# Nine pairs of weight strips of a mixer's input projection, each pair as seven half-size block products

## The chip, the cores and the metric

The kernel runs on one core of a Trainium2 chip. The metric is the device time of one execution in microseconds, as the median of several runs. Engines: TensorE (matmuls, "PE" in the profile; its weight loads are "PEld"), VectorE ("DVE"), ScalarE ("ACT"), GpSimd ("POOL") and SyncE ("SP"), which issues nearly all transfers to and from the memory, in one queue and in order.

## The reference

One decoder layer over 1024 rows of 1024 features, all in float32:

```python
f1 = swiglu(rms_norm(h, ffn1_pre_g[l]), ffn1_w_in[l], ffn1_w_out[l])
h = h + HALF_STEP * rms_norm(f1, ffn1_post_g[l])

u = rms_norm(h, mix_pre_g[l])
p_rwkv, p_swa, q_mem, gate_logits = _split(u @ w_in[l], IN_SIZES)
...
g_a, g_b, g_c = _split(jax.nn.sigmoid(gate_logits + gate_b[l]), (D, D, D))
merged = (g_a * (y_a @ w_branch[l, 0]) + g_b * (y_b @ w_branch[l, 1])
          + g_c * (y_c @ w_branch[l, 2]))
h = h + rms_norm(merged @ w_out[l], mix_post_g[l])

f2 = swiglu(rms_norm(h, ffn2_pre_g[l]), ffn2_w_in[l], ffn2_w_out[l])
h = h + HALF_STEP * rms_norm(f2, ffn2_post_g[l])
```

`swiglu` has an inner width of 2816. `y_a` is a recurrent mixing of rows (RWKV-7), `y_b` attention in a window of 128 with 8 query heads, `y_c` attention to 256 memory rows. The change is in `u @ w_in[l]`: its output has 48 strips of 128 columns. Strips 0 to 13 feed the recurrence, 14 to 19 the window attention (`p_swa`), 20 to 23 are the memory queries, and 24 to 47 the gates ("gate 0" is strip 24).

## The kernel before, in words

**Operands.** A float32 product is made of three matmuls. Each weight strip of 128 x 512 is loaded (`w_raw`), rounded by ScalarE to `w_hi` (L288) and its rest `w_lo` subtracted by VectorE (L290); activations are split the same way (`split`, L472 and L473). `mm3` (L364 to L366) multiplies hi by hi, hi by lo and lo by hi into one PSUM tile of 128 x 512. A strip of `w_in` has 8 row blocks of the inner dimension and two halves of the rows, so it takes 8 x 2 x 3 = 48 matmuls. `plan` writes the order of all weight strips down in one list; loads, roundings and subtractions run up to eight operands ahead of the matmuls that use them.

**Half-size products.** The two feed-forward blocks (ffn1, ffn2) already take two strips at once: of the four quarter blocks of the weights and of the activations, sums and differences are formed, so that seven products of 12 matmuls (`product`) do the work of eight. In ffn1's and ffn2's input stage the sums of the weights are formed as the strips arrive; 22 pairs run there, 19 us each (84 matmuls). For the output weights of ffn1 and ffn2 the sums are formed once, in units of four loads, four VectorE operations and four stores to `ffn1_sum_d` and `ffn2_sum_d` (`sums_loads`, `sums_made`): eleven units of ffn1 beside its input pairs 9 to 19 (tiles `ws`, L655 to L658), eleven of ffn2 in the attention stage and the branches (`sums_beside`, tiles `gin`).

**The mixer, in order of TensorE.** ffn1's output products end with the norm of the mixer's input (`pre_norm`), which leaves `u` split. Strips for the recurrence follow (`rwkv_prep`), then strips 14 to 17 and 20 to 23 (`att_block`, PSUM tile `pq`; of 14 and 15 only the second half of the rows) and gates 0 to 7 (`gate_block`, tile `pgate`). Beside these VectorE inverts the recurrence's triangular blocks, row by row (`rwkv_invert`, L1129 and L1130, 62 pairs of operations that depend on each other): a load `inv<-ab_d` of 2 MB begins it, a store to `inv_d` ends it. The recurrence's chain of 16 chunks (`rwkv_chain`) comes next, with gates 8 and 9 as filling matmuls between its short steps. Then eight blocks of the memory attention (matmuls `msc`, `mptr`, `mpv`) and eight of the window attention (`sc`, `ptr`, `pv`), each mixed with a number of filling matmuls (`LUMPS`) out of the remaining gates and the first two branch products (`pb`).

**Branches, projection, ffn2.** The third branch and the output projection follow: eight strips for each half of the rows (`out_projection`, tile `pw`). While the second half is multiplied, VectorE and ScalarE take the first half through the post-norm, the residual sum (L874, L877) and ffn2's pre-norm (L526), whose results are split (L473) for ffn2's first products (tile `px`). Each norm sums squares (L482, L486), passes them through two matmuls (`ps_rs`, L459) and a square root (L462 to L466): a "statistic". Four of them lie here, two for each half.

**What sets the order.** A scheduler orders the instructions of each engine when the program is built, by the priorities and pins in the code and a model of each engine; on the chip every engine, and the transfer queue, runs its list strictly in order, each instruction behind its waits. Tiles come from pools; a pool that opens where another has closed waits for the other's last users.

## Time and profile before

| | |
|---|---|
| median of 3 runs | 2263.78 us (2262.43 to 2265.75) |
| profiled execution, span | 2260.2 us |
| TensorE busy | 2236.6 us, 11876 matmul records |
| VectorE busy | 1652.0 us |
| ScalarE busy | 1000.2 us |
| transfers | 417.66 MB, 185 GB/s on average |

The profile is of one execution of its own; its span lies 3.6 us under the median of the runs. Rows of a timeline give a start, a duration, the engine, the line of the kernel and the operation with its tiles (`out<-in`). Matmul rows overlap: what one costs in a stream is the step from start to start. A row of the windows gives a stretch of time and each engine's busy time in it, then the granted clock of TensorE, the busy share of the transfer engines and the rate they moved.

### The profile page before, as it was taken

The page shows a single profiled execution, that of the slowest core. Times are in us where ns is not written, and L with a number is a line of the kernel's source. Part 1 is how long each engine was busy: PE and PEld are TensorE (multiplying, and loading weights), DVE is VectorE, ACT ScalarE, POOL GpSimd, SP SyncE. Part 2 cuts the span into 40 slices and gives each one's busy share as a digit, 9 for nine tenths or more (in the row PEclk, how much of TensorE's full clock was granted, in tenths as well). Part 3 has the DMA queues.
Part 4 walks back from the last instruction along what each step waited for, and adds up shares of the span by engine and source line. Part 5 has one row for each costly group of instructions (what it writes and reads, how often), then busy time and mean ns, then how long its engine had stood idle before and what let it go on. Part 6 is the DMA issues. An engine that isn't in the chain of part 4 may idle for free.

```text
span 2260.2 us, 33447 instructions
## 1 busy us (share of the span) xinstructions
PE 2236.6 (99%) x11876; PEld 1840.4 (81%) x11876; DVE 1652.0 (73%) x2719; ACT 1000.2 (44%) x1880; POOL 58.1 (3%) x114
## 2 busy tenths in 40 slices
PE   8999999999999999999999999999999999999998
PEld 6888888888888788888888887788888888888887
DVE  6987777666698886995666576684898885656576
ACT  6533333454556653223454445334663233345451
POOL 0000000000000000001320000000000000000000
PEclk9999999999999999999999999999999999999999
DMA  8465666686654467325438885654565542347663
GB/s 291 157 210 168 215 212 208 214 276 207 191 173 149 117 143 183 118 93 194 144 113 289 266 278 186 209 177 136 173 214 188 189 168 90 116 165 250 204 196 122
DMA packets 280775, 417.66 MB, mean 185 GB/s; under 512 B 82304, under 2 KB 104320, under 8 KB 280352
## 3 DMA queue, kind: packets, MB, share of 16 engines
q1 hardware_dynamic: 272832, 400.26, 55.3%
q10 hardware_dynamic: 7776, 15.28, 2.0%
q8 instruction: 93, 1.52, 0.3%
q14 instruction: 74, 0.61, 0.1%
HBM read 284.89 MB, written 129.50 MB: 183 GB/s over the span
## 4 chain that ended last, share of the span: by engine, by line
PE 93%; DVE 4%; DMA 1%; ACT 1%; issue 1%; SPq 0%; DVEq 0%; ACTq 0%
PE px L365 7%; PE px L364 7%; PE px L366 7%; PE po L365 6%; PE po L366 6%; PE po L364 6%; PE pgate L364 4%; PE pgate L366 4%; PE pgate L365 4%; PE pz L365 3%; PE pz L364 3%; PE pz L366 3%; PE pb L364 2%; PE pb L365 2%; PE pb L366 2%; PE pr L364 2%
## 5 line engine op out<-in xcount | busy, mean ns | idle before, releaser
L288 ACT CAST w_hi<-w_raw 128x512 fp32r<-128x512 f32 x594 | 367.5, 620 | 734.5 <-PE px L365 159.7
L290 DVE TENSOR_TENSOR w_lo<-w_raw,w_hi 128x512 fp32r<-128x512 f32 x594 | 407.6, 687 | 196.0 <-ACT w_hi L288 175.2
L366 PE MATMUL po<-u,w_lo 128*128 128x512 f32 (+1 forms) x476 | 180.9, 380 | 0.0
L364 PE MATMUL po<-u,w_hi 128*128 128x512 f32 (+1 forms) x476 | 180.9, 380 | 0.0
L365 PE MATMUL po<-u,w_hi 128*128 128x512 f32 (+1 forms) x476 | 180.9, 380 | 0.0
L364 PE MATMUL pgate<-u,w_hi 128*128 128x512 f32 x384 | 153.2, 399 | 0.0
L366 PE MATMUL pgate<-u,w_lo 128*128 128x512 f32 x384 | 151.4, 394 | 0.0
L365 PE MATMUL pgate<-u,w_hi 128*128 128x512 f32 x384 | 149.8, 390 | 0.0
L365 PE MATMUL px<-f,w_hi 128*128 128x512 f32 x352 | 137.2, 390 | 1.0 <-DVE f L473 1.0
L364 PE MATMUL px<-u,w_hi 128*128 128x512 f32 x352 | 137.0, 389 | 0.8 <-DVE km L1442 0.8
L364 PE MATMUL px<-f,w_hi 128*128 128x512 f32 x352 | 137.1, 389 | 0.1
L366 PE MATMUL px<-u,w_lo 128*128 128x512 f32 x352 | 137.0, 389 | 0.0
L366 PE MATMUL px<-f,w_lo 128*128 128x512 f32 x352 | 137.0, 389 | 0.0
L365 PE MATMUL pz<-u,w_hi 128*128 128x512 f32 x352 | 137.0, 389 | 0.0
L365 PE MATMUL px<-u,w_hi 128*128 128x512 f32 x352 | 136.9, 389 | 0.0
L364 PE MATMUL pz<-u,w_hi 128*128 128x512 f32 x352 | 136.9, 389 | 0.0
L366 PE MATMUL pz<-u,w_lo 128*128 128x512 f32 x352 | 136.9, 389 | 0.0
L473 DVE TENSOR_TENSOR u<-hid,u 128x512 fp32r<-128x512 f32 x114 | 78.3, 690 | 46.5 <-ACT u L472 43.5
L364 PEld LDWEIGHTS po<-u,w_hi 128*128 128x128 f32 x476 | 89.5, 188 | 17.1
L365 PEld LDWEIGHTS po<-u,w_hi 128*128 128x128 f32 x476 | 89.5, 188 | 17.1
L366 PEld LDWEIGHTS po<-u,w_lo 128*128 128x128 f32 x476 | 89.5, 188 | 16.8
L472 ACT CAST u<-hid 128x512 fp32r<-128x512 f32 x114 | 70.7, 620 | 64.3 <-DMA hid<-form_d 55.7
(401 smaller groups left out, 5097.4 us busy)
## 6 DMA issues: line engine op xcount, KB each, us to landing
w_raw<-in_ffn_in SPq DMA_DIRECT2D x220, 256.0 KB
hid<-form_d SPq DMA_DIRECT2D x154, 256.0 KB
w_raw<-in_win SPq DMA_DIRECT2D x112, 256.0 KB
form_d<-g SPq DMA_DIRECT2D x88, 256.0 KB
w_raw<-ffn_sum_d SPq DMA_DIRECT2D x88, 256.0 KB
form_d<-h SPq DMA_DIRECT2D x66, 256.0 KB
w_raw<-in_ffn_out SPq DMA_DIRECT2D x66, 256.0 KB
gate_d<-gate SPq DMA_DIRECT2D x24, 512.0 KB
```

The source lines that it names most:

```text
L288: self.nc.scalar.copy(hi, x)
L290: self.split_last = self.nc.vector.tensor_tensor(lo, x, hi.bitcast(F32), ALU.subtract)
L364: mm(out, wh, xh, start=first, stop=False, **kw)
L365: mm(out, wh, xl, start=False, stop=False, **kw)
L366: self.last_mm = mm(out, wl, xh, start=False, stop=last, **kw)
L472: self.nc.scalar.copy(hi, x)
L473: self.nc.vector.tensor_tensor(lo, x, hi.bitcast(F32), ALU.subtract)
```

## The change

Strips 20 to 23 and gates 0 to 13 are now multiplied in nine pairs (`WIN_PAIRS`), each as seven products of 12 matmuls, in `win_pair`. For that:

- `mix_forms` makes four sums and differences of the quarters of the normed input and splits them (16 operations and 16 splits). The normed rows come back from a new buffer `xn_d`, written by `pre_norm` (16 stores) and loaded by `mix_x` (16 loads, tiles `part`).
- The sums of the weights (`win_sum_d`) are formed in nine more units: eight as second units beside ffn1's pairs 9 to 16, one beside pair 20.
- The stores of all these sums are issued later (`sums_store`): behind the loads of the next pair's `t2` operand.
- Before the chain now lie 14 gates (`GATES_FIRST`), and three (14 to 16) belong to the chain's stage (`GATES_EARLY` = 17), where there were two. Seven gates remain for the attention stage, where there were fourteen, and its fills per block go from 30 and 54 matmuls to 18 and 36.
- Seven of ffn2's units of sums stay in attention; four move into the first half of the output projection.

```diff
-GATES_EARLY = 10
-LUMPS = (30, 54)
-GATES_FIRST = 8
+GATES_EARLY = 17
+LUMPS = (18, 36)
+GATES_FIRST = 14
+ATT_PLAIN = (16, 17)
+ATT_PAIRS = ((20, 21), (22, 23))
+WIN_PAIRS = ATT_PAIRS + tuple((24 + g, 25 + g) for g in range(0, GATES_FIRST, 2))
+SECOND_UNITS = 8
+UNITS_EARLY = 7
...
@@ ffn_in
-                if f == "ffn1" and FIRST[f] <= j < FIRST[f] + KP:
-                    self.sums_made(f, j - FIRST[f], self.sums_loads(f, j - FIRST[f], self.sums_tiles(pool)), made)
+                if f == "ffn1" and j >= FIRST[f]:
+                    i = j - FIRST[f]
+                    if i < SECOND_UNITS:
+                        self.sums_made("win", i, self.sums_loads("win", i, self.sums_tiles(pool, f"sq{TH}")), self.up)
+                    what = (f, i) if i < KP else ("win", i - KP + SECOND_UNITS)
+                    if what[0] == f or what[1] < len(WIN_PAIRS):
+                        self.sums_made(*what, self.sums_loads(*what, self.sums_tiles(pool)), made)
+                    if j == KF - 1:
+                        self.sums_store()
...
+    def mix_forms(self, u, pool, parts, first):
+
+        V = self.nc.vector
+        tile = lambda: pool.tile([P, TH], F32R, tag="mix_form", name="mix_form", bufs=8 * KH)
+        fs = {"b11": [u[k][0] for k in range(KH)]}
+        for n, h in (("b21", 0), ("b22", 1)):
+            fs[n] = [u[k][h] for k in range(KH, KD)]
+        for n in ("t2", "t1", "t3", "t4"):
+            fs[n] = [(tile(), tile()) for _ in range(KH)]
+        with self.tc.high_priority(offset=self.lead):
+            for k in range(KH):
+                x12, x22, x11, x21 = self.mix_x(k, parts) if k else first
+                V.tensor_tensor(x22, x22, x12, ALU.subtract)
+                V.tensor_tensor(x12, x12, x11, ALU.subtract)
+                V.tensor_tensor(x11, x22, x11, ALU.add)
+                V.tensor_tensor(x21, x21, x11, ALU.subtract)
+                for n, x in (("t2", x11), ("t1", x12), ("t3", x22), ("t4", x21)):
+                    self.split(x, *fs[n][k])
+        return fs
...
+        part(0, "b11", px, True)
+        x = kept(px)
+        part(1, "b21", py, True, True)
+        made(0, first, 0, py, x)
+        part(2, "t2", px)
+        u1 = kept(px)
+        part(3, "t1", pz, True)
+        z = kept(pz)
+        part(4, "t3", px)
+        made(1, second, 1, px, z)
+        part(5, "b22", pz, False, True)
+        made(0, first, 1, pz, u1)
+        part(6, "t4", px, False, True)
+        made(1, second, 0, px)
...
@@ mixer
-                self.rwkv_invert(pool, ab_d, inv_d)
-            for f in ATT_BLOCKS[ATT_FIRST:]:
-                self.att_block(f, u, att_d, lambda: gp.tile([P, T], F32, tag="gate", name="att", bufs=2))
-            for g in range(GATES_FIRST):
-                self.gate_block(g, u, gp, gate_d)
+                fs = self.mix_forms(u, forms, parts, first)
+                for f in FILL[ATT_FIRST:] + ATT_PLAIN:
+                    self.att_block(f, u, att_d, out)
+                self.rwkv_invert(pool, ab_d, inv_d)
+                for i in range(len(WIN_PAIRS)):
+                    self.win_pair(i, fs, parts, out, att_d, gate_d)
...
-                self.units = self.sums_beside()
+                self.units = self.sums_beside(range(UNITS_EARLY))
...
-                self.attention(blocks, [42, 34] + [LUMPS[0]] * (nb - 2) + [LUMPS[1]] * nb, {0: [tables], 1: [keys], 2: [load_values], 4: [turn_values]})
+                self.attention(blocks, [26, 20] + [LUMPS[0]] * (nb - 2) + [LUMPS[1]] * nb, {0: [tables], 1: [keys], 2: [load_values], 3: [turn_values]})
...
@@ build
-                for _ in self.out_projection(merged, x, 0):
-                    pass
+                with tc.tile_pool(reuse_waits="tile", name="units", bufs=4) as self.widepool:
+                    self.units = self.sums_beside(range(UNITS_EARLY, KP))
+                    for i, _ in enumerate(self.out_projection(merged, x, 0)):
+                        if i % 16 == 15:
+                            self.unit()
+                    assert next(self.units, None) is None
```

Here `kept` copies a PSUM tile by ScalarE, `made` adds a kept copy to a PSUM tile by VectorE and, for gates, applies the tanh. Where the order of instructions moves, in three places (each row: line, operation, tiles, shape, and in brackets the engines and transfers it waits for).

SyncE at the beginning of the inverse, before; `att_d` is the buffer of strips 14 to 23:

```order
L1497 DMA att_d<-att 128x512 [waits DMAHW2_49,Activation_49]
L1124 DMA inv<-ab_d 128x4096 [waits DMAHW3_49,DMAHW6_49,PE_49,Pool_49]
L279 DMA w_raw<-in_win 128x512 [waits DMAHW4_49,DVE_49]
L1497 DMA att_d<-att 128x1024 [waits DMAHW5_49,Activation_49]
L279 DMA w_raw<-in_win 128x512 [waits DVE_49]
```

and with the change:

```order
L1600 DMA att_d<-att 128x512 [waits DMAHW7_49,Activation_49]
L1155 DMA inv<-ab_d 128x4096 [waits DMAHW0_49,DMAHW3_49,PE_49,Pool_49]
L1338 DMA part<-xn_d 128x512 [waits DMAHW1_49,DVE_49]
L1338 DMA part<-xn_d 128x512 [waits DMAHW2_49,DVE_49]
L1338 DMA part<-xn_d 128x512 [waits DVE_49]
L1338 DMA part<-xn_d 128x512 [waits DMAHW4_49,DVE_49]
L292 DMA w_raw<-win_sum_d 128x512 [waits DMAHW5_49]
L292 DMA w_raw<-win_sum_d 128x512 [waits DMAHW6_49,DVE_49]
L1600 DMA att_d<-att 128x1024 [waits DMAHW7_49,Activation_49]
L1338 DMA part<-xn_d 128x512 [waits DMAHW0_49,DVE_49]
```

The loads of the normed rows of blocks 1 to 3 now stand between the inverse's load and the weight loads.

VectorE in the middle of the inverse, before:

```order
L1129 TENSOR_TENSOR itmp<-inv 128x860 [waits DVE_49]
L1130 TENSOR_TENSOR inv<-inv,itmp 128x20x43 [waits DVE_49]
L1129 TENSOR_TENSOR itmp<-inv 128x882 [waits DVE_49]
L290 TENSOR_TENSOR w_lo<-w_raw,w_hi 128x512 [waits DMAHW7_49,PE_49,Activation_49]
L1130 TENSOR_TENSOR inv<-inv,itmp 128x21x42 [waits DVE_49]
L1129 TENSOR_TENSOR itmp<-inv 128x902 [waits DVE_49]
L1130 TENSOR_TENSOR inv<-inv,itmp 128x22x41 [waits DVE_49]
```

and with the change:

```order
L1160 TENSOR_TENSOR itmp<-inv 128x860 [waits DVE_49]
L1382 TENSOR_TENSOR att<-py,part 128x512 [waits DMAHW0_49,PE_49,Activation_49]
L303 TENSOR_TENSOR w_lo<-w_raw,w_hi 128x512 [waits DMAHW6_49,Activation_49]
L1161 TENSOR_TENSOR inv<-inv,itmp 128x20x43 [waits DVE_49]
L1160 TENSOR_TENSOR itmp<-inv 128x882 [waits DVE_49]
L1161 TENSOR_TENSOR inv<-inv,itmp 128x21x42 [waits DVE_49]
L303 TENSOR_TENSOR w_lo<-w_raw,w_hi 128x512 [waits DMAHW7_49,PE_49,Activation_49]
L1160 TENSOR_TENSOR itmp<-inv 128x902 [waits DVE_49]
L303 TENSOR_TENSOR w_lo<-w_raw,w_hi 128x512 [waits DMAHW1_49,PE_49,Activation_49]
L1161 TENSOR_TENSOR inv<-inv,itmp 128x22x41 [waits DVE_49]
```

The steps of the inverse now alternate with operand subtractions and with sums of products, and the latter wait for TensorE.

VectorE in the output projection, from the end of half 0 to the first statistic, before:

```order
L486 TENSOR_TENSOR sq<-sq 128x512 [waits DVE_49,Activation_49]
L290 TENSOR_TENSOR w_lo<-w_raw,w_hi 128x512 [waits DMAHW2_49,PE_49,Activation_49]
L290 TENSOR_TENSOR w_lo<-w_raw,w_hi 128x512 [waits DMAHW3_49,PE_49,Activation_49]
L486 TENSOR_TENSOR sq<-sq 128x512 [waits DVE_49,Activation_49]
L290 TENSOR_TENSOR w_lo<-w_raw,w_hi 128x512 [waits DMAHW4_49,PE_49,Activation_49]
L290 TENSOR_TENSOR w_lo<-w_raw,w_hi 128x512 [waits DMAHW5_49,PE_49,Activation_49]
L486 TENSOR_TENSOR sq<-sq 128x512 [waits DVE_49,Activation_49]
L454 SCALAR_TENSOR_TENSOR sq_lo<-sq,eps,sq_hi 128x512 [waits Activation_49]
```

and with the change:

```order
L679 TENSOR_TENSOR gin<-gin 128x512 [waits DMAHW7_49,DVE_49]
L303 TENSOR_TENSOR w_lo<-w_raw,w_hi 128x512 [waits DMAHW5_49,PE_49,Activation_49]
L303 TENSOR_TENSOR w_lo<-w_raw,w_hi 128x512 [waits DMAHW1_49,PE_49,Activation_49]
L499 TENSOR_TENSOR sq<-sq 128x512 [waits DMAHW6_49,DMAHW5_49,Activation_49]
L499 TENSOR_TENSOR sq<-sq 128x512 [waits DVE_49,Activation_49] x2
L303 TENSOR_TENSOR w_lo<-w_raw,w_hi 128x512 [waits DMAHW4_49,PE_49,Activation_49]
L499 TENSOR_TENSOR sq<-sq 128x512 [waits DVE_49,Activation_49] x2
L303 TENSOR_TENSOR w_lo<-w_raw,w_hi 128x512 [waits DMAHW0_49,PE_49,Activation_49]
L499 TENSOR_TENSOR sq<-sq 128x512 [waits DVE_49]
L467 SCALAR_TENSOR_TENSOR sq_lo<-sq,eps,sq_hi 128x512 [waits Activation_49]
```

The sums of squares of half 0, which stood one after each strip, now stand together behind the last unit of sums, and the first of them waits for transfers.

106 lines of the change are left out of this document (81 added, 25 removed).

## The prediction

> **What bounds the kernel now.** First the page's busy times and its slices, then the chain that ended last:
>
> ```profile
> PE 2236.6 (99%) x11876; PEld 1840.4 (81%) x11876; DVE 1652.0 (73%) x2719; ACT 1000.2 (44%) x1880; POOL 58.1 (3%) x114
> PE   8999999999999999999999999999999999999998
> DVE  6987777666698886995666576684898885656576
> PEclk9999999999999999999999999999999999999999
> GB/s 291 157 210 168 215 212 208 214 276 207 191 173 149 117 143 183 118 93 194 144 113 289 266 278 186 209 177 136 173 214 188 189 168 90 116 165 250 204 196 122
> PE 93%; DVE 4%; DMA 1%; ACT 1%; issue 1%; SPq 0%; DVEq 0%; ACTq 0%
> ```
>
> TensorE is busy almost everywhere, at the full granted clock, and owns 93% of the chain. So a matmul taken away is worth its step, as long as the other engines keep up with a TensorE that asks sooner. A step is read from TensorE's timeline, first and last of 15 rows in a row without a wait:
>
> ```profile
> 954.81 0.39 PE L365 MATMUL pq<-u,w_hi 128*128 128x512 f32 x1
> ...
> 957.99 0.39 PE L364 MATMUL pq<-u,w_hi 128*128 128x512 f32 x1
> ```
>
> 14 steps in 3.18 us: 0.227 us each (the 0.39 us of a row overlap). Second, how much room the other engines have in the stages touched (columns: busy us of TensorE, weight load, VectorE, ScalarE, GpSimd, then clock, DMA share, GB/s):
>
> ```profile
> 240.00:280.00 40.00, 40.00 (x179) 33.11 (x178) 28.45 (x46) 14.41 (x26) 0.00 (x0) 1.00 0.66 219
> 450.00:500.00 50.00, 49.89 (x220) 41.00 (x219) 30.40 (x62) 25.23 (x45) 0.25 (x4) 1.00 0.86 278
> 908.40:1029.20 120.80, 120.80 (x535) 100.02 (x534) 117.31 (x147) 26.88 (x45) 0.00 (x0) 1.00 0.28 96
> 1200.00:1300.00 100.00, 98.42 (x526) 84.13 (x525) 63.14 (x123) 48.06 (x116) 0.96 (x1) 1.00 0.83 275
> 1300.00:1447.00 147.00, 147.00 (x795) 116.52 (x793) 103.44 (x248) 74.68 (x236) 0.00 (x0) 1.00 0.66 213
> 1574.30:1649.30 75.00, 75.00 (x329) 61.22 (x328) 65.96 (x105) 49.82 (x90) 0.00 (x0) 1.00 0.57 187
> ```
>
> In order: ffn1's pairs, ffn1's end, the inverse beside the mixer input, the memory blocks, the window blocks, the last part of the out projection. VectorE is full beside the inverse and at 88% in the projection; DMA is near its end around 450 and 1250.
>
> What a VectorE operation costs in a stream, from VectorE's timeline; the first two depend on each other, the rest do not:
>
> ```profile
> 1577.67 0.69 DVE L465 SCALAR_TENSOR_TENSOR sq<-ps_rs,sq 128x512 f32<-128x512 f32 x1 [0.84 <-ACT sq L464]
> 1578.39 0.69 DVE L466 SCALAR_TENSOR_TENSOR rs<-sq,rs 128x512 f32<-128x512 f32 x1
> 1611.31 0.68 DVE L473 TENSOR_TENSOR u<-acc,u 128x512 fp32r<-128x512 f32 x1
> 1611.91 0.68 DVE L473 TENSOR_TENSOR r<-acc,r 128x512 fp32r<-128x512 f32 x1
> 1612.51 0.68 DVE L290 TENSOR_TENSOR w_lo<-w_raw,w_hi 128x512 fp32r<-128x512 f32 x1
> 1613.11 0.68 DVE L473 TENSOR_TENSOR u<-acc,u 128x512 fp32r<-128x512 f32 x1
> ```
>
> 0.72 us from start to start where one waits for the other, 0.60 where not.
>
> **The change part by part.**
>
> *Matmuls removed.* Nine pairs of 96 matmuls become 84 (seven products of 12): 108 fewer, and the order has exactly 108 fewer of 128x512 (8726 for 8834). 108 x 0.227 = **-24.5 us**. Everything below is a price for it.
>
> *The pair stage (att 20 to 23, gates 0 to 13).* VectorE here also runs the inverse:
>
> ```profile
> L1130 DVE TENSOR_TENSOR inv<-inv,itmp 128x62 f32<-128x62 f32 (+30 forms) x62 | 53.2, 859 | 1.8
> L1129 DVE TENSOR_TENSOR itmp<-inv 128x62 f32<-128x62 f32 (+30 forms) x62 | 53.2, 858 | 2.3 <-DMA inv<-ab_d 0.7
> L1129 DVE TENSOR_TENSOR itmp<-inv x62: 224/942/1191, 908.4 to 1028.6; 128x62 f32<-128x62 f32 x2, 128x122 f32<-128x122 f32 x2, 128x180 f32<-128x180 f32 x2, 128x236 f32<-128x236 f32 x2
> 1574.28 0.39 PE L459 MATMUL ps_rs<-sq_hi,mean_r 128*128 128x512 f32 x1
> 918.37 0.33 SPq L1497 DMA_DIRECT2D att_d<-att  x1
> ```
>
> The inverse is 106.4 us of durations, some 100 with the overlap. The change puts between its first and last operation 24 of the forms' operations, 66 operand subtractions (24 before) and the 27 sums of the products: about 171 us of VectorE at 0.60 to 0.72 each. It starts at 908.4 and so ends near 1080; TensorE, from strip 17's end at 918.4 (the store's row), reaches the same place of its order after some 161 us, at 1079. The two are level, with eight operands of lead between them. Of each pair VectorE has 10 own operations (6.0 us) and 12 to 14 of the inverse, 18.2 to 19.7 us against 84 x 0.227 = 19.0. At the stage's start the forms of rows 1 to 3 are late: their loads stand on SP behind the inverse's 2 MB load, which took 9.6 us (issued 898.8 before), and I count the last forms at 930 to 932 where TensorE asks at 929 to 931. I take **+4**; 0 if the lead covers all, +11 if every operation costs its whole 0.68. ScalarE's 27 copies and 16 casts lie in an engine that was busy 27 of 121 us: 0.
>
> *ffn1's pairs 9 to 16.* Each gets a second unit of sums: 4 loads, 4 subtractions, 4 stores of 256 KB.
>
> ```profile
> ws<-in_ffn_out SPq DMA_DIRECT2D x44, 256.0 KB
> ffn_sum_d<-ws SPq DMA_DIRECT2D x44, 256.0 KB
> ```
>
> VectorE: 28.45 us in 40 is 13.5 a pair; 4 x 0.60 more makes 16 of 19. The queue is tighter: 8 x 262 KB in 19.04 us is 110 GB/s on top of 219, 329 in all. The rows at a share of 0.66 to 0.86 scale to 323 (278/0.86) to 332 (219/0.66) at a full queue, so it just fits; a deficit of up to 0.4 us a pair is under the lead. I take **+2**, for the second unit's subtractions stand in front of the `up` sums, and VectorE waits there if a load is late. Low end 0; high end 20, if the queue gives no more than the 291 GB/s of the page's best slice (below). [...] No row here shows more than 291.
>
> *Mixer's norm and the chain.* The chain's first matmul stands here:
>
> ```profile
> 1047.84 0.56 PE L1145 MATMUL y<-center,f 64*64 64x64 f32 x12
> ```
>
> The 16 stores of the normed rows are waited for by no one before the pairs. The chunk loop keeps six gate matmuls a chunk; the third gate's stand ahead of it (29) and behind it (19). The inverse ends some 50 us later, but so does TensorE reach the chain: six more gates lie before it. Between the two are 10 us of pairs and 29 gate matmuls (6.6 us), 17 us for a store and reload that had 19 (the inverse's last start, 1028.6 above, to 1047.8). Without this cover the wait would be some 7 us. Taken as 0.
>
> *Attention.* Seven gates fewer are left for it, so a block's fills go from 30 to 18 and from 54 to 36.
>
> ```profile
> L132 DVE TENSOR_REDUCE st<-sc 128x8 f32<-128x1024 f32 x8 | 9.7, 1215 | 0.2
> DVE gin L655 <- DMA gin<-in_ffn_out: 13.7, 4, 6.6
> PE msc L94 <- DVE gin L655: 1.6, 1, 1.6
> ```
>
> Eight reductions, so eight window blocks in 147 us: 18.4 each for TensorE, 12.9 of busy VectorE. Eighteen matmuls fewer is -4.1 us: 14.3 at most for TensorE, and 17.2 - 4.1 = 13.1 in a short one. VectorE drops the 1.5 subtractions of those fills and four of the eleven units of sums: about 11.5 to 12.5, but unevenly (I count 10.5 to 16 in a block), and the round from turns to copies, exponentials, normalising and turns is 9 to 10 us in series. The one stall of before (1.6 us, a sum behind its load) may stay. **+3**, 0 to 12.
>
> *Out projection.* The four moved units (16 loads, 16 subtractions, 16 stores) come into half 0, and the tiles of the first statistic's sums take the units' space, so they wait for the last unit's stores. By the order the first statistic comes 43 matmuls (9.8 us) later, and only 284 matmuls (64.4 us) instead of 323 (73.2) lie from it to the fourth:
>
> ```profile
> 1599.15 0.50 PE L459 MATMUL ps_rs<-sq_hi,mean_r 128*128 128x512 f32 x1
> 1614.33 0.39 PE L364 MATMUL px<-u,w_hi 128*128 128x512 f32 x1
> ```
>
> VectorE's work there hardly shrinks (102 operations for 106, 66 us of busy time for 75 us), with 4 to 6 us of waiting in the statistics' own chains: 70 to 72 us against 64.4. The place: before, 15.2 us lay from the second statistic to ffn2's first `px`, filled by 62 `pw`; now 21 matmuls, 4.8 us, while the first `u` came 12.2 us after the statistic (1611.31, above). That is 7.4 of stall. **+7**, 0 if VectorE catches up earlier, 10 if the stores come late too.
>
> Sum: -24.5 + 4 + 2 + 3 + 7 = **-8.5 us** against the profiled span of 2260.2, 2251.7; the median of the runs, 2263.8, lies 3.6 above that span, so **2255**.
>
> **The rivals.**
>
> *The covers hold.* Stalls do not add: a VectorE that is late once finds the next stage waiting. Pairs 1, ffn1 0, attention 0, projection 5: -18.5, **2245**. For it speaks that TensorE's waits in the whole of ffn1 are one of 1.0 us:
>
> ```profile
> PE px L365 <- DVE f L473: 1.0, 1, 1.0
> ```
>
> Against it: VectorE's 117 of 121 us beside the inverse.
>
> *VectorE becomes the bound.* In the pair stage half the operations follow one they depend on or wait for a product; if each costs 0.69 instead of 0.60, the 171 us are 186 and the pairs cost 11; in the window blocks it then costs 5. 11 + 2 + 5 + 7 = 25: no gain, **2264**. It decides once the mean step passes 0.65 us. [...]
>
> *Slower: the DMA queue in ffn1.* If the queue moves no more than the best slice, 291 GB/s, a pair's 6.27 MB take 21.5 us, 2.5 more than TensorE, eight times: 20. With 14 to 16 elsewhere: +10, **2274**. It decides from some 300 GB/s down (1.9 us a pair). Loads, sums and stores share one queue in order, so late operands stop TensorE itself. Against it: 0.86 of the queue at 450 to 500 left TensorE 49.89 of 50.
>
> **How the numbers follow.** Forecast 0.45 (2249 to 2261), covers hold 0.22, VectorE 0.22, queue 0.11. The range 2242 to 2268 leaves out about 0.07 below and 0.12 above. Of this kernel's time 0.2% (4.5 us) is what can be told from no change: faster 0.69 (0.40 + 0.22 + 0.07), same 0.19 (0.05 + 0.12 + 0.02), slower 0.12.
>
> **What would show it.** Right: 8726 wide matmuls; VectorE full from 908 to about 1080 and TensorE with a few us of waits there, most at the first pair; a wait of some 7 us of TensorE for `u` at ffn2's first `px`; less than 1 us a pair in ffn1, with the DMA share near 1. Wrong: waits for operands in ffn1 above 5 us (queue), window blocks above 14 us (VectorE), or a projection without that wait.

## The result, and the profile after

| | before | with the change |
|---|---|---|
| median of the runs beside each other | 2263.11 us (2262.42 to 2265.75, 4 runs) | 2279.3 us (2276.13 to 2285.0, 4 runs) |
| ratio, 95% interval | | 1.0074 [1.0057, 1.0092] |
| profiled execution, span | 2260.2 us | 2283.0 us |

The change makes the kernel 16 us slower, where 2255 was forecast. The profiled execution is the slowest of the four (2285.0 in the list of times), so its losses, below, are a few us larger than the median's. From the page of the changed kernel, busy times, slices and the chain:

```profile
PE 2233.8 (98%) x11768; PEld 1828.0 (80%) x11768; DVE 1717.0 (75%) x2841; ACT 1036.4 (45%) x1944; POOL 60.1 (3%) x114
DVE  6987877766698986899566668785898885656676
GB/s 287 156 208 184 295 302 274 227 297 213 190 220 197 135 139 172 206 139 152 231 141 104 280 246 217 174 200 281 139 230 172 193 177 93 116 157 247 213 194 120
PE 81%; DVE 9%; DMA 6%; issue 2%; ACT 2%; SPq 1%; DVEq 0%; ACTq 0%
```

The 108 matmuls are gone (11768 records for 11876), but TensorE's busy time fell by 2.8 us only instead of 24.5, and its share of the chain went from 93% to 81%. So TensorE waits more, and beside that its remaining matmuls take longer. What it waits for, from its view of the waits (us in total, times, longest):

```profile
PE px L377 <- ACT u L749: 7.0, 6, 3.2
PE sc L99 <- DVE pt L167: 4.8, 3, 2.5
PE px L378 <- DVE u L486: 4.0, 1, 4.0
PE msc L99 <- DVE gin L676: 3.3, 1, 3.3
PE mpv L99 <- DVE sc L133: 2.7, 1, 2.7
PE y L1176 <- DMA f<-pk_d: 1.5, 1, 1.5
PE px L377 <- ACT part L1375: 1.4, 1, 1.4
```

In order: ffn1's pairs, the window blocks, ffn2's first product in the projection, a memory block behind a sum of ffn2's weights, a memory block's last matmuls behind VectorE's work for a window block, the chain's first step, the first pair of the mixer input.

To price each stage, TensorE's timeline is cut at the first matmul of a named product (first `px` of ffn1's sums, first `po`, first `pq`, the chain's first `y`, first `msc`, first `sc`, last `pv`, first `pw`, the first statistic of the projection, ffn2's first `pz` and `po`). A stage's loss is its duration, less its duration before, less 0.2267 us for each wide matmul that it has more than before (or plus, for each fewer). The table gives it for every kernel of this document in us; "window blocks" includes the little that is left of attention behind the last `pv`'s cut, and "all" is the sum over all stages from the first cut on, to be set against the 24.5 us that the missing matmuls gain. e10 isn't in it: its profiled execution took 7702 us, where its other ten runs took 2264 to 2269.

| kernel | ffn1 pairs | ffn1 out | mixer pairs | memory blocks | window blocks | projection | all |
|---|---|---|---|---|---|---|---|
| the change | 10.1 | 0.8 | 6.3 | 4.3 | 15.7 | 9.5 | 46.5 |
| e1 | -0.1 | 1.2 | 6.5 | 3.6 | 13.5 | 10.3 | 34.5 |
| e2 | 4.5 | 1.3 | 8.7 | 5.1 | 13.3 | 9.3 | 43.9 |
| e3 | 6.5 | 0.6 | 6.3 | 3.4 | 17.5 | 10.4 | 43.1 |
| e4 | 7.1 | 1.4 | 6.6 | 4.2 | 16.8 | 0.0 | 35.1 |
| e5 | 0.0 | 1.1 | 6.3 | 4.1 | 12.4 | 10.5 | 34.5 |
| e6 | 6.5 | 1.4 | 6.2 | -1.8 | 0.8 | 0.0 | 13.5 |
| e7 | 0.0 | 6.5 | 5.8 | 4.8 | 17.3 | 0.0 | 36.2 |
| e8 | -0.7 | 7.8 | 6.1 | 5.3 | 14.3 | 0.0 | 34.1 |
| e9 | 5.4 | 8.8 | 6.5 | -0.6 | 1.1 | 0.0 | 24.5 |
| e11 | 4.7 | 8.3 | 3.6 | -1.4 | 0.7 | 0.2 | 20.8 |
| e12 | 6.1 | 1.3 | 6.5 | -1.5 | 5.2 | 0.1 | 17.5 |
| e13 | 8.2 | 1.6 | 6.4 | 5.5 | 12.7 | 0.8 | 34.5 |
| e14 | 0.6 | 9.8 | 2.9 | -2.0 | 1.2 | 0.0 | 12.5 |
| e15 | 7.2 | 1.3 | 6.8 | 0.2 | 5.3 | -0.1 | 23.9 |
| e16 | -0.6 | 0.0 | 6.3 | -1.9 | 0.8 | 0.0 | 5.4 |

46.5 less 24.5 is 22.0, and the spans differ by 22.8, of which 0.7 lie ahead of the first cut: the stages account for the loss. Attention lost 20.0 us, ffn1's pairs 10.1, the projection 9.5, the pairs of the mixer input 6.3. A single profile carries some noise here: ffn1's pairs are the same code in the change, e3, e4, e6, e12, e13 and e15, and lose 6.1 to 10.1.

**ffn1's pairs.** Windows of 19 us, one pair each, before (columns as in the prediction, the last three the granted clock, the DMA share and GB/s):

```profile
259.00:278.00 19.00, 19.00 (x86) 15.73 (x85) 13.97 (x24) 7.05 (x13) 0.00 (x0) 1.00 0.64 202
335.00:354.00 19.00, 19.00 (x85) 15.73 (x85) 13.95 (x23) 7.05 (x13) 0.00 (x0) 1.00 0.61 201
```

and with the change:

```profile
259.00:278.00 19.00, 19.00 (x85) 15.73 (x85) 14.34 (x24) 6.14 (x11) 0.00 (x0) 1.00 0.91 311
335.00:354.00 19.00, 17.65 (x79) 14.28 (x78) 14.01 (x23) 6.86 (x12) 0.00 (x0) 1.00 0.89 304
404.00:408.00 4.00, 4.00 (x12) 3.13 (x11) 2.09 (x4) 0.54 (x2) 0.00 (x0) 0.57 1.01 358
```

TensorE loses nothing up to some 300 us, where the pairs live on their lead; behind it up to 1.4 us a pair, and 3.2 in the last of them. VectorE is not full there (14 of 19 us). From 240 to 400 us it waits for loads (the first two rows), and the queue in its turn stands at stores that wait for VectorE (the other two, the queue's own waits):

```profile
DVE w_sum L328 <- DMA w_raw<-in_ffn_in: 16.6, 4, 5.7
DVE ws L676 <- DMA ws<-in_win: 10.0, 4, 3.2
...
SPq L713 <- DVE g L767: 12.4, 4, 6.6
SPq L689 <- DVE ws L678: 12.0, 15, 1.1
```

From 259 to 373 us the queue stays at 303 to 313 GB/s over a pair, with a share of 0.88 to 0.91, where the pairs ask for 329. That isn't the end of the transfer engines, as other stretches of 19 us show, the first at the beginning of the chain in the kernel before, the second among the window blocks with the change:

```profile
1030.00:1049.00 19.00, 19.00 (x105) 15.58 (x104) 2.54 (x4) 4.72 (x8) 1.58 (x4) 1.00 1.02 360
1340.00:1359.00 19.00, 19.00 (x126) 16.08 (x125) 10.82 (x26) 8.24 (x25) 0.00 (x0) 1.00 1.01 348
```

So 303 to 313 is what the queue held in this stage, not a limit of it; whether the transfers' rate or the order of the queue, with its waits for VectorE, sets it is not shown here. Shorter stretches lie above the 19 us rows, too (461 GB/s over the 4 us from 1089.5 with the change).

**The clock.** The same row shows the second part of the loss: a granted clock of 0.57. TensorE's timeline behind its wait of 3.2 us:

```profile
403.46 0.50 PE L377 MATMUL px<-f,w_hi 128*128 128x512 f32 x1 [3.20 <-ACT u L749]
...
404.45 0.63 PE L377 MATMUL px<-f,w_hi 128*128 128x512 f32 x1
404.88 0.63 PE L378 MATMUL px<-f,w_hi 128*128 128x512 f32 x1
405.30 0.63 PE L379 MATMUL px<-f,w_lo 128*128 128x512 f32 x1
```

The steps are 0.42 to 0.43 us instead of 0.227, for 3.4 us: the pause cost 1.6 more behind it. The granted clock behind the other four long waits (3.3, 4.0, 2.7 and 2.5 us), in rows of the windows:

```profile
1309.00:1315.00 6.00, 5.31 (x13) 4.26 (x14) 4.12 (x7) 0.51 (x3) 0.00 (x0) 0.50 0.67 236
1635.00:1641.00 6.00, 5.69 (x16) 4.41 (x17) 5.79 (x11) 2.73 (x6) 0.00 (x0) 0.61 0.00 0
1364.90:1370.90 6.00, 5.93 (x38) 5.35 (x39) 6.00 (x18) 1.58 (x3) 0.00 (x0) 1.00 0.58 170
1388.00:1394.00 6.00, 5.83 (x26) 4.51 (x26) 5.96 (x19) 2.26 (x10) 0.00 (x0) 1.00 0.86 296
```

The half clock follows the three waits of 3.2 us and more, and not those of 2.7 and 2.5. It also stands once, from 1434.9 to 1441.7, behind a wait of 1.3 us in the window blocks; none follows those of 1.3 to 1.4 in ffn1 and in the first pair of the mixer input. Between the kernel's first 40 and last 12 us these four stretches, the first of 3.4 us and the others of 6.8, hold 38 wide matmuls, whose longer steps cost the changed kernel 7.8 us; the kernel before has no such stretch (a granted clock of 1.00 from 40 to 2248 us). What sets the half clock off, and what ends it, is not shown here. In e16, where TensorE waits at most 2.2 us once past the kernel's first load, some matmuls of the pairs of the mixer input took 0.63 us, too. So the length of a wait alone doesn't tell whether the half clock follows.

**Attention.** TensorE's rows of the scores `sc` tell the blocks' pace; the second to the fifth window block with the change:

```profile
1355.85 2.10 PE L99 MATMUL sc<-kd,qs 64*128 64x256 f32 x16
1372.04 2.10 PE L99 MATMUL sc<-kd,qs 64*128 64x256 f32 x16
1384.56 1.14 PE L99 MATMUL sc<-kd,qs 64*128 64x256 f32 x8
1388.17 1.73 PE L99 MATMUL sc<-kd,qs 64*128 64x256 f32 x8 [2.47 <-DVE pt L167]
1401.22 1.14 PE L99 MATMUL sc<-kd,qs 64*128 64x256 f32 x8
```

The blocks start 16.2, 12.5 and 16.7 us apart; the scores of the fourth stop in their middle (so do the fifth's, for a shorter time). Ahead of the largest pause VectorE's timeline has this row, a sum of ffn2's weights in front of the memory block's work:

```profile
1308.89 0.69 DVE L676 TENSOR_TENSOR gin<-gin 128x512 f32<-128x512 f32 x1 [5.00 <-DMA gin<-in_ffn_out]
```

**Projection.** The first statistic, and ffn2's second `px`, in TensorE's timeline:

```profile
1597.90 0.50 PE L472 MATMUL ps_rs<-sq_hi,mean_r 128*128 128x512 f32 x1 [1.13 <-ACT sq_hi L466]
...
1635.31 0.80 PE L378 MATMUL px<-u,w_hi 128*128 128x512 f32 x1 [4.00 <-DVE u L486]
```

Between the `pw`'s end at 1629 and 1635 TensorE has four `px` to multiply, no more.

**Pairs of the mixer input.** The last step of the inverse and the last split of the forms (duration least, median and most, first and last start), and a form's matmul in the stream:

```profile
L1161 DVE TENSOR_TENSOR inv<-inv,itmp x62: 223/933/1186, 920.1 to 1088.1; 128x62 f32<-128x62 f32 x2, 128x122 f32<-128x122 f32 x2, 128x180 f32<-128x180 f32 x2, 128x236 f32<-128x236 f32 x2
L486 DVE TENSOR_TENSOR mix_form<-part,mix_form x16: 683/685/693, 908.1 to 944.7; 128x512 fp32r<-128x512 f32 x16
L378 PE MATMUL px<-mix_form,w_hi x19: 387/392/398, 1013.2 to 1039.5; 128*128 128x512 f32 x19
```

The split forms were ready at 945, 13 us later than I had counted, of which 11.5 is the later start of the stage (the inverse's first operation stands at 919.9 for 908.4): in the stage's own time the forms are some 2 us late, and the inverse ends at 1088 where 1080 and 11.5 had been expected. VectorE in between, in a row of the windows:

```profile
919.50:1098.00 178.50, 177.11 (x769) 143.88 (x768) 167.83 (x236) 78.32 (x131) 0.00 (x0) 1.00 0.52 171
```

It is almost full, and TensorE waits for it 1.4 us only. That wait isn't for a form to multiply: TensorE waits for ScalarE's copy of the first product (`part`, L1375), and the copy had waited 2.7 us for VectorE to finish the split of a form. What cost more than foreseen is the form's matmul (e11).

### The profile page after: what moved, and what is told of

Read it like the earlier page. It is cut to its first block, busy times and chain, and to the rows that moved or that the text cites. A ratio compares the mean times of both kernels' runs of the same rounds, so it can differ in the third digit from the quotient of the medians.

```text
span 2283.0 us, 33721 instructions
## 1 busy us (share of the span) xinstructions
PE 2233.8 (98%) x11768; PEld 1828.0 (80%) x11768; DVE 1717.0 (75%) x2841; ACT 1036.4 (45%) x1944; POOL 60.1 (3%) x114
## 4 chain that ended last, share of the span: by engine, by line
PE 81%; DVE 9%; DMA 6%; issue 2%; ACT 2%; SPq 1%; DVEq 0%; ACTq 0%
PE px L378 8%; PE px L377 8%; PE px L379 8%; PE po L378 6%; PE po L377 6%; PE po L379 6%; PE pz L378 4%; PE pz L377 4%; PE pz L379 4%; PE pr L377 2%; PE pr L378 2%; PE pr L379 2%; DVE w_lo L303 2%; PE pgate L377 1%; PE pgate L378 1%
## 5 line engine op out<-in xcount | busy, mean ns | idle before, releaser
L301 ACT CAST w_hi<-w_raw 128x512 fp32r<-128x512 f32 x621 | 384.2, 620 | 722.6 <-PE px L378 194.0
L303 DVE TENSOR_TENSOR w_lo<-w_raw,w_hi 128x512 fp32r<-128x512 f32 x621 | 427.1, 689 | 156.4 <-ACT w_hi L301 137.6
L378 PE MATMUL px<-u,w_hi 128*128 128x512 f32 x388 | 152.1, 392 | 4.0 <-DVE u L486 4.0
L377 PE MATMUL px<-u,w_hi 128*128 128x512 f32 x388 | 151.4, 392 | 1.9 <-ACT u L485 1.1
L379 PE MATMUL px<-u,w_lo 128*128 128x512 f32 x388 | 151.8, 391 | 0.0
L377 PE MATMUL pz<-u,w_hi 128*128 128x512 f32 x388 | 151.0, 389 | 0.0
L378 PE MATMUL pz<-u,w_hi 128*128 128x512 f32 x388 | 151.0, 389 | 0.0
L379 PE MATMUL pz<-u,w_lo 128*128 128x512 f32 x388 | 151.0, 389 | 0.0
L378 PEld LDWEIGHTS px<-u,w_hi 128*128 128x128 f32 x388 | 73.2, 189 | 20.2 <-DVE u L486 4.9
L377 PEld LDWEIGHTS px<-u,w_hi 128*128 128x128 f32 x388 | 73.2, 189 | 18.4 <-ACT r L485 1.6
L377 PE MATMUL pr<-u,w_hi 128*128 128x512 f32 x224 | 87.8, 394 | 0.0
```

The lines of the kernel that those rows point to most:

```text
L301: self.nc.scalar.copy(hi, x)
L303: self.split_last = self.nc.vector.tensor_tensor(lo, x, hi.bitcast(F32), ALU.subtract)
L377: mm(out, wh, xh, start=first, stop=False, **kw)
L378: mm(out, wh, xl, start=False, stop=False, **kw)
L379: self.last_mm = mm(out, wl, xh, start=False, stop=last, **kw)
```

## The experiments

In each stage the question is what holds TensorE: the transfers of the units of sums, VectorE's operations, or space that comes free late. Each diff is against the changed kernel unless another is named; ratios are against the kernel before, run beside.

**e1: ffn1 without the second units.** The pairs of the mixer input multiply plain quarter blocks instead of their sums.

```diff
-            return (a1, a2, *(self.win_sum_d[n, m] for m in (1, 0, 2, 3)), b2)[q]
+            return (a1, a2, a1, b2, a2, a1, b2)[q]
...
-                    if i < SECOND_UNITS:
-                        self.sums_made("win", i, self.sums_loads("win", i, self.sums_tiles(pool, f"sq{TH}")), self.up)
```

> The eight second units beside ffn1's pairs 9 to 16 are left out (loads, subtractions and stores), and the pairs of the mixer multiply plain quarter blocks of the weights in place of their sums: the same number of loads and matmuls. In the profile of the change, ffn1's input stage lost 10.1 us. If the second units are its whole cause, whether by traffic or by VectorE, those 10 us come back: about 2269 us, ffn1's first output product at 460 us as before. If the loss came from the sums' later stores or from the ninth unit, under 3 us come back.

Measured: 2273.5 us, 1.0043 [1.0028, 1.0058]. ffn1's loss is gone (-0.1 in place of 10.1), so the second units make it; by the medians 5.8 us come back, since the changed kernel's profile is of its slowest run. 13.5 in the window blocks and 10.3 in the projection stay, so those are not its echo.

**e2 and e5: transfers or subtractions?** e2 keeps the second units' loads and stores and leaves their four subtractions out:

```diff
+        second = f == "win" and q < SECOND_UNITS
...
+            if not second:
+                V.tensor_tensor(a22, a21, a22, ALU.add)
...
```

> The second units keep their 64 transfers, but their four subtractions each are left out (the stores write back what was loaded). Theory queue: the transfers fill the queue and the weights land late; nothing changes, 2276 to 2280 us, ffn1's input stage 9 to 11 us longer than before. Theory VectorE: 32 operations of 0.60 us less, the stage is at most 3 us longer than before, 2270 to 2273 us.

e5 keeps the subtractions, on tiles that are there anyway, and leaves the 64 transfers out:

```diff
-                        self.sums_made("win", i, self.sums_loads("win", i, self.sums_tiles(pool, f"sq{TH}")), self.up)
+                        a = self.sums_tiles(pool, f"sq{TH}")
...
+                            for n, t in enumerate(a):
+                                V.tensor_tensor(t, w, w, ALU.subtract)
```

> The second units' 32 subtractions stay on VectorE, at the same places, but on tiles that are in place already; their 64 transfers are left out, and the pairs of the mixer multiply plain quarter blocks. Transfers alone cost 4.8 us of ffn1's input stage, both together 6.5 to 10.8 in three profiles. Theory queue: without the transfers the weights land in time and VectorE has room (16 of 19 us a pair): the stage is under 1 us longer than before. Theory VectorE: 3 us or more remain.

Measured: e2 2281.8 us, 1.0074 [1.0056, 1.0091], ffn1's pairs lose 4.5; e5 2273.0, 1.0042 [1.0027, 1.0057], they lose 0.0. One window of ffn1, e2:

```profile
240.00:400.00 160.00, 157.18 (x688) 128.21 (x687) 111.53 (x179) 56.60 (x100) 0.00 (x0) 1.00 0.87 300
```

and e5:

```profile
240.00:400.00 160.00, 160.00 (x708) 132.60 (x707) 131.40 (x214) 59.39 (x102) 0.00 (x0) 1.00 0.65 221
```

With 131 of 160 us VectorE is no bound: without the transfers nothing is lost. The loss needs the transfers, though e2's 4.5 lie between what its two theories named. The rest, up to the 6.1 to 10.1 of the full unit, is put down by argument only: a late load also holds VectorE, whose sums stand behind it, and with them the stores.

**e3 and e8: more fills in the window blocks.** e3: fills of 50 matmuls in each. e8, on e7 (below): more fills in some blocks, fewer behind.

```diff
-LUMPS = (18, 36)
+LUMPS = (18, 50)
```

> Only the number of filling matmuls of a window block, 50 for 36; the matmuls come out of the tail behind the last block, so their sum is the same. Theory: a window block of 36 fills is shorter for TensorE than VectorE's round, and TensorE's pauses there, with the stretches at half clock behind them, cost 15.7 us in the profile; with 50 fills 12 to 15 of them come back, about 2265 us. Rival, late loads of the sums' units: the pauses stay where the loads are, 0 to 4 us come back.

```diff
-..., [26, 20] + [LUMPS[0]] * (nb - 2) + [LUMPS[1]] * nb, ...
+..., [26, 20, 18, 36, 18, 18, 18, 18, 50, 46, 40, 40, 36, 36, 36, 36], ...
```

> As the run before, and the fills of the blocks are distributed anew out of the same sum: 36 in the fourth memory block, and 50, 46, 40, 40 and four times 36 in the window blocks, 54 fewer in the tail. The two long pauses, at the fourth memory block (3.5 us and half clock) and at the turn to the window blocks (2.8 us), are where the added fills go: if cover is what lacks there, 5 to 9 us come back, 2261 to 2266 us. If the late loads hold VectorE whatever TensorE has to do meanwhile, the pauses move behind the fills and under 2 us come back.

Measured: e3 2284.8 us, 1.0094 [1.0076, 1.0113], above both theories: the window blocks lose 8.7 instead of 15.7, but 8.8 appear behind them, where the fills have run out. e8: 2272.5, 1.0040 [1.0025, 1.0055], 3.4 us under e7, between its two theories; 14.3 of loss in place of 17.3. With the matmuls that are left, the order of the fills moves most of the pauses elsewhere; what makes the blocks late must go.

**e4: the four units back from the projection into attention.**

```diff
-UNITS_EARLY = 7
+UNITS_EARLY = 11
...
-                    for i, _ in enumerate(self.out_projection(merged, x, 0)):
-                        if i % 16 == 15:
-                            self.unit()
...
+                for _ in self.out_projection(merged, x, 0):
+                    pass
```

> All eleven units of ffn2's sums in attention as before, none in the projection; TensorE's order in attention is the same. Theory, space and place of the first statistic: the projection gives back 9 us (the wait for ffn2's first products falls from 4 us to under 0.5), and attention, with four more units in blocks where VectorE is the bound, loses 2 to 5: 2273 to 2276 us. Rival, the projection is short of cover whatever the units do: it gives back under 3 us, 2279 us or more.

Measured: 2278.3 us, 1.0066 [1.0049, 1.0083], above the forecast. In the profile the projection's 9.5 us are gone and attention loses one more. The medians differ by one us only, the profiled spans, 2272.4 and 2283.0, by ten: e4's profile is of the shortest of its runs (2274.5 to 2279.4), the changed kernel's of its longest. So what the four units cost in attention can't be read from these two profiles to a few us.

**e13: the four units stay in the projection, in space of their own.** Their pool stays open until the statistics are done, so that the tiles of the statistic's sums open elsewhere.

```diff
-                with tc.tile_pool(reuse_waits="tile", name="units", bufs=4) as self.widepool:
+                apart = contextlib.ExitStack()
+                self.widepool = apart.enter_context(tc.tile_pool(reuse_waits="tile", name="units", bufs=4))
...
+                apart.close()
```

> The change as it is, with its four units in the projection's first half, but the pool of their tiles stays open until the norms' pool closes, so the two lie in different places. In the order of TensorE the first statistic then stands after 213 matmuls of the projection, as before, in place of 256. Theory space: the 9.5 us of the projection come back, 2268 to 2272 us. Rival, the units' work: the wait for ffn2's first products stays above 3 us, 2276 us or more.

Measured: 2272.6 us, 1.0037 [1.0023, 1.0050]; the projection loses 0.8. Its first statistic follows the matmuls without a wait, after as many `pw` as before the change:

```profile
1584.28 0.40 PE L379 MATMUL pw<-u,w_lo 128*128 128x512 f32 x1
1584.51 0.40 PE L472 MATMUL ps_rs<-sq_hi,mean_r 128*128 128x512 f32 x1
```

So neither the units' transfers nor their sums cost there; that the statistic's tiles waited for the units' space did.

**e6, e12, e15: what attention pays for.** All three stand on e4, with plain quarter blocks in ffn2's output products. e6 leaves ffn2's units out altogether; e12 keeps their 44 subtractions without a transfer; e15 keeps loads and subtractions and leaves the 44 stores out.

```diff
+        if f == "ffn2" and a in SUMS:
+            return self.io[f + "_out"][SUMS.index(a), q]
...
-                self.units = self.sums_beside(range(UNITS_EARLY))
+                self.units = iter(())
```

> As the run with all units in attention, but no unit of ffn2's sums is formed at all: ffn2's output products multiply plain quarter blocks in place of the sums. Attention keeps its 18 and 36 fills a block. It lost 20 us in the change (4.3 in the memory blocks, 15.7 in the window blocks). Theory, late loads of the units hold VectorE: 12 us or more of it come back, 2260 to 2266 us. Theory, the blocks' own round is longer than 36 fills: under 6 us come back, 2270 us or more. In between, both.

> All units in attention as in that run, but without their 88 transfers: the 44 subtractions stay on VectorE, at the same places, on a tile that is there already, and ffn2's output products multiply plain quarter blocks. Theory, late loads hold VectorE: attention's loss (20 us with units, -1 without any) falls under 5 us, about 2255 us. Theory, VectorE's own time: 10 us or more remain, 2262 us or more.

```diff
-            for x, t in zip(parts, a):
+            for x, t in zip(parts, a) if f != "ffn2" else ():
...
+        if f == "ffn2":
+            w = self.sg[:, :TH].rearrange("p (k c) -> p k c", c=P)
+            with self.tc.issue_after(behind.ins):
+                for t in (a22, a21, a11, a12):
+                    V.tensor_tensor(t, w, w, ALU.subtract)
+            return
```

and, for e15,

```diff
+                if f == "ffn2":
+                    continue
```

(in the loop that issues the stores.)

> All units in attention as in that run, with their loads and subtractions but without their 44 stores; ffn2's output products multiply plain quarter blocks. With stores attention lost 21 us, without any transfer 3.7. Theory, the loads themselves land late and hold VectorE: 12 us or more of loss remain, 2267 us or more. Theory, the stores block the queue and the tiles: under 8 remain, 2262 us or less.

Measured: e6 2251.5 us, 0.9949 [0.9933, 0.9966], below both its theories; e12 2258.8, 0.9982 [0.9970, 0.9993]; e15 2261.0, 0.9989 [0.9980, 0.9998]. Memory and window blocks together lose -1.0 with nothing, 3.7 with the subtractions, 5.5 with the loads too, and 21.0 with the stores too (e4). So of 22 us VectorE's work makes 4.7, the loads 1.8, the stores 15.5, each added to what stands in this order; the medians of the whole kernels give 7.3, 2.2 and 17.3. The first operation of a unit shows how the stores do it, in e4 and in e15 (the last figure is VectorE's idle time before it, and what ended it):

```profile
L676 DVE TENSOR_TENSOR gin<-gin 128x512 f32<-128x512 f32 x11 | 7.5, 685 | 15.3 <-DMA gin<-in_ffn_out 15.3
L678 DVE TENSOR_TENSOR gin<-gin 128x512 f32<-128x512 f32 x11 | 7.5, 683 | 0.1
```

With the stores VectorE waits 15.3 us for the units' loads, without them 0.1: the stores make the loads late. A store takes its place in the one queue, and it keeps its tile until it has landed: in e4's attention the queue waits three times, 5.5 us in all, for such a landing before it issues a unit's load; in the changed kernel's ffn1 (240 to 400 us) it does so four times, 2.5 us in all. Which of the two weighs more isn't told apart here.

**e7: second units of ffn1 at every other pair** (9, 11, 13, 15, 17, 19, 20), on e4.

```diff
-SECOND_UNITS = 8
+SECOND_AT = (9, 11, 13, 15, 17, 19, 20)
...
-                    if i < SECOND_UNITS:
+                    if j in SECOND_AT:
```

> All ffn2 units in attention, and the second units of the mixer's weights spread over ffn1's pairs 9, 11, 13, 15, 17, 19 and 20 (two more as the only unit of 20 and 21) in place of 9 to 16: a pair with two units is mostly followed by a pair with one, 5.2 MB a pair on average (274 GB/s). Theory queue: the stage's loss falls from 6.5 to 10.8 us to under 2, 2268 to 2272 us. Rival, a double pair costs its 1.2 us wherever it stands: 7 us remain, 2275 us.

Measured: 2275.9 us, 1.0052 [1.0037, 1.0067]. The pairs lose nothing; 6.5 us appear in ffn1's output products, which wait for their `hid` loads (ScalarE 18.7 us in 13 waits from 455 to 520); that these stand behind the units of pairs 20 and 21 in the queue is argued. e16, below, has the same second units up to pair 19, one unit at pair 20 and none at 21, and loses nothing in either stage: a queue that falls behind in one pair recovers in the next.

**e9, e10: ffn2's units beside ffn2's own pairs** 13 to 21, as ffn1's are, two left in attention. e9 is the change with it (second units of ffn1 at pairs 9, 10, 12, 13, 15, 16, 18); e10 the kernel before with it alone.

```diff
-UNITS_EARLY = 7
+UNITS_EARLY = 2
...
-                if f == "ffn1" and j >= FIRST[f]:
+                if j >= FIRST[f]:
...
+                    else:
+                        what = (f, UNITS_EARLY + i)
```

> Nine of ffn2's eleven units of sums move out of attention to ffn2's own input pairs 13 to 21, one beside each as ffn1 has them; two stay in attention, none is in the projection. The second units of the mixer's weights stand at ffn1's pairs 9, 10, 12, 13, 15, 16 and 18. Ledger by the runs so far: matmuls -24.5, ffn1 0 to 2, pair stage +6, attention -1 to +2 (without any unit it was -1.0), projection 0, ffn2's pairs 0 to 2 (VectorE was busy 88 of 144 us there and the queue moved 112 GB/s), end 1: 2244 to 2252 us, faster than before. If a unit costs its loads wherever it stands, ffn2's pairs lose 5 us or more and it is 2255 us or more.

> The kernel before, with nine of ffn2's eleven units of sums moved from attention to ffn2's pairs 13 to 21 in the same way. Attention's blocks are long there (30 and 54 fills), and its only pause that a unit made was 1.7 us with the slow steps behind it. Theory, units hurt only where the blocks are short: 0 to -3 us, 2260 to 2263 us. If the units cost as much beside long fills: -10 us or more.

Measured: e9 2260.6 us, 0.9988 [0.9980, 0.9997]; e10 2267.1, 1.0013 [1.0004, 1.0022]. In e9 the blocks lose 0.5 instead of 21.0. It still missed its forecast by over 8 us: ffn1's pairs lost 5.4 and its output products 8.8, and 4.1, in no column of the table, ffn2's output products. e10 is slower than both its theories. In the kernel before TensorE's stalls in attention were one of 1.6 us, at full granted clock behind it, so that the fills of 30 and 54 covered the rest and the move had little to gain; what it cost there no profile shows. The move pays only with the change.

**e11: the forms elsewhere in SBUF.** e9 with 896 bytes per partition in front of the forms. The forms' matmuls had steps of 0.233 us where all others have 0.227; their tiles begin 1120 bytes past a multiple of 2048, the tiles of `u` and `f` 2016 past one. With the pad the forms lie at 2016, too.

```diff
+                nc.gpsimd.memset(forms.tile([P, 224], F32, name="pad", bufs=1), 0.0)
```

> As the run with units in ffn2's pairs, but the tiles of the mixer's forms lie 896 bytes further up in each partition (at 2016 modulo 2048 like the activations elsewhere, in place of 1120). Matmuls that stream these tiles had a step of 0.2328 to 0.2333 us, all others 0.2267. If the place of the tile is the cause, their step becomes 0.2267 and the 432 matmuls give 2.6 us back, 2242 to 2250 us; if it is what they are multiplied with or what runs beside them, the step stays.

Measured: 2258.9 us, 0.9977 [0.9969, 0.9986]; the time missed the forecast as e9's did, but the step is 0.2269 (mean of over 400 matmuls) for 0.2330, and the pairs of the mixer input lose 3.6 instead of 6.5. The place is the cause. Nor is 2016 the only good one: the tiles `form` of ffn1's output products begin 1248 or 1760 bytes past a multiple of 2048, and their matmuls have steps of 0.227. The durations, which had been 387 to 398 ns, are even:

```profile
L378 PE MATMUL px<-mix_form,w_hi x18: 389/389/389, 1014.2 to 1039.4; 128*128 128x512 f32 x18
```

**e14, e16: the change with its side work placed anew.** e14, on e11: second units of ffn1 at pairs 9, 11, 13, 15, 17, the other four of `w_in`'s units as halves beside ffn1's output products 1 to 4; four of ffn2's units in the projection with space of their own, seven beside ffn2's pairs, none in attention.

```diff
-SECOND_AT = (9, 10, 12, 13, 15, 16, 18)
-UNITS_EARLY = 2
+SECOND_AT = (9, 11, 13, 15, 17)
+UNITS_EARLY = 4
...
+                halves = self.win_half_units(q) if f == "ffn1" and 1 <= n and q < len(WIN_PAIRS) else iter(())
+                for s, _ in enumerate(self.ffn_out_steps(f, n, hid, acc)):
+                    if s in (0, 20, 40):
+                        next(halves, None)
...
-                self.units = self.sums_beside(range(UNITS_EARLY))
+                self.units = iter(())
...
+                for i, _ in enumerate(self.out_projection(merged, x, 0)):
+                    if i % 16 == 15 or i == 8:
+                        self.unit()
```

> All of it together: the mixer's second units at ffn1's pairs 9, 11, 13, 15 and 17 and, as half units, three in ffn1's output products; four of ffn2's units in the projection's first half in a space of their own, seven at ffn2's pairs 13 to 19, none in attention; pairs 20 and 21 free in both; the forms' tiles shifted by 896 bytes. Ledger: matmuls -24.5, ffn1 0 to 3, its output products 1 to 4, pair stage +3.6, attention -1, projection 0 to 1, ffn2 0 to 2: 2242 to 2254 us, the middle at 2247. If the output products of ffn1 cannot take the half units: 2256 us or more.

Measured: 2253.8 us, 0.9956 [0.9943, 0.9968]: faster than before. 9.8 of the 12.5 us that it still loses lie in ffn1's output products, 6.4 of them in one wait. The mean granted clock of the profiled execution is 0.996, where e16's is 0.998; how much of the other 3.4 is slower steps isn't told apart here. The waits there:

```profile
PE ps_rs L472 <- ACT sq_hi L466: 6.6, 2, 6.4
DVE ws L851 <- DMA ws<-in_win: 14.2, 4, 5.0
ACT u L485 <- DMA hid<-form_d: 44.6, 36, 6.6
```

By these waits the half units stand on VectorE ahead of the norm's squares and wait there for their loads. e16, on e14, moves one of the four back to ffn1's pair 19 as a second unit, one to pair 20 alone, and leaves two, in halves, beside the products 1 and 2.

```diff
-SECOND_AT = (9, 11, 13, 15, 17)
+SECOND_AT = (9, 11, 13, 15, 17, 19)
...
-                q = len(SECOND_AT) + n - 1
+                q = len(SECOND_AT) + n
```

> As e14_all_units_placed, but the second units of in_win that stood in ffn1's output products are moved back among ffn1's pairs (pairs 9, 11, 13, 15, 17, 19 and 20), so that only two half units remain in the output products n=1 and n=2; nothing is left out. Theory (the output stage of e14 lost 9.8 us because hid, ws and the squares queue behind the units' transfers and additions there): that loss falls to 1 to 3 us, the pairs lose 0 to 3, and the time is 2244 to 2250. Rival (the output stage loses whatever stands in it, as e7 lost 6.5 with units at pairs 19 and 20): it still loses 6 to 9 us and the time stays at 2251 to 2256.

Measured: **2243.0 us (2239.9 to 2246.5), 0.9909 [0.9895, 0.9923]**. The output products lose 0.0, all stages 5.4, and 24.5 less 5.4 is 19.1, where the profiled spans differ by 19.0 (2241.2 for 2260.2). Two of its 19 us windows in ffn1's pairs, one with a second unit and one without:

```profile
335.00:354.00 19.00, 19.00 (x85) 15.75 (x84) 15.54 (x26) 7.46 (x14) 0.00 (x0) 1.00 0.68 227
354.00:373.00 19.00, 19.00 (x85) 15.75 (x84) 14.31 (x24) 7.03 (x13) 0.00 (x0) 1.00 0.93 322
```

TensorE is full in both. Its window blocks are 12.5 to 13.4 us apart:

```profile
1350.88 2.10 PE L99 MATMUL sc<-kd,qs 64*128 64x256 f32 x16
1363.37 2.10 PE L99 MATMUL sc<-kd,qs 64*128 64x256 f32 x16
1376.76 2.10 PE L99 MATMUL sc<-kd,qs 64*128 64x256 f32 x16
```

And what TensorE still waits for longest, beside the kernel's first load, is the copy of the first pair's first product and the chain's first load:

```profile
PE px L377 <- ACT part L1402: 2.2, 1, 2.2
PE y L1203 <- DMA f<-pk_d: 1.5, 1, 1.5
```

The first `px<-mix_form` matmul (927.5) stands behind the first of these waits. Such matmuls took up to 635 ns, as at the granted clock of 0.50 in the changed kernel, where their median is 389; and the pairs of the mixer input lose 6.3 again, where e14 lost 2.9.

## Why the prediction was wrong, step by step

- **Matmuls removed, -24.5: right.** 108 fewer, at 0.2267; e16's account closes on it to 0.1 us.
- **Pair stage +4: 6.3.** VectorE did keep up: it was busy 168 us of the 178 from the inverse's start on, and TensorE's one wait for it is at the first pair (1.4 us), where I had put it, though for a copy that waits for a form's tile and not for a late form. Of the rest, nine pairs of 48 matmuls by 0.006 us are 2.7 of slower steps that nothing in the trace of before could show, and 1.5 is the chain's first load, which I had taken as 0.
- **ffn1's pairs +2, "so it just fits": the first step that failed.** 329 GB/s were set against a rate scaled to a share of 1. In a row of such pairs the queue held a share of 0.88 to 0.91 and 303 to 313 GB/s, 16 to 26 too few, which is 0.9 to 1.5 us of the 19 in each pair. The high end, 20, had the transfers as its cause (the queue rival), and was too dear: 6.1 to 10.1. Nor is the best slice, 291, an end of the queue: a slice is 56 us long, and the kernel before moved 360 GB/s over 19 us (1030 to 1049). Neither rate told what these pairs would get.
- **Attention +3, 0 to 12: the step that decided.** It lost 20.0. I priced the blocks by VectorE's busy time, and the units there by their four subtractions. These are 4.7 us of 22 (e12). Their stores make 15.5, by making the units' loads late (e4, e15). Before they stood in the same blocks without harm, for the fills covered a late block: TensorE was busy 147.00 of 147 us in the window blocks. VectorE's waits for these units' loads hardly grew; in the prediction they were 13.7 us in four for eleven units, with all eleven in attention (e4) they are 15.3, and with the change's seven:

```profile
DVE gin L676 <- DMA gin<-in_ffn_out: 10.4, 5, 5.0
```

What grew is the part of them that TensorE feels: 1.6 us before, the 3.3 and more above now. And the sign that I had set for VectorE as the bound, blocks above 14 us, came true (16.2 and 16.7) with the stores as its main cause.
- **Projection +7: the mechanism right, 9.5.** The first statistic came late because its tiles wait for the units' space (e13: 0.8 without this), and TensorE ran out of `pw` before ffn2's first products. The wait is 4.0 and not 7.4 us long at its longest; the slow steps behind it add some 2.
- **Not in the sum at all: the clock.** I priced each wait by its length. Behind those of 3.2 us and more, and once behind a short one, TensorE ran at half the rate for 3.4 to 6.8 us: 7.8 us in the whole, which are part of the losses above.
- **Rivals.** The queue one (2274, chance 0.11) named the nearest time, and that was luck: it put 20 us into ffn1's pairs and 14 to 16 elsewhere, where 10.1 and 36 were lost. The VectorE one fell: e5 and e12 show its operations at 0.0 and 4.7. "Stalls do not add", from the covers rival, is contradicted too: ffn1, attention and projection lost independently of one another (e1, e4, e6).

The median's loss, 16.2 us, is smaller than the 22.8 of the profiled execution, since that was the slowest of the four; by the median the stages lost 41 rather than 47.

## What to carry to other kernels

A change that takes work off the bounding engine takes the cover off all that ran beside it (here the window blocks, where TensorE was busy 147.00 of 147 us before, lost 15.7): price each side task (its loads, operations and stores) in the stage where it stands with the *new* length of the stage, and spread it so that no two neighbours overfill the queue. A queue that serves loads and stores in order should be counted at the rate it has been seen to hold with the same mix of transfers, not at the rate scaled to full (here 303 to 313 GB/s for 323 to 332). And before a change is dropped as slower, place its side work anew: the same arithmetic went from 1.0074 to 0.9909.
